# A decoder trunk: the sums of a short phase copied out by two engines and added later, more shared columns in the short phases, and gathered rows held five deep

## The chip, the cores and the metric

The kernel runs on one core of a Trainium2 chip, in one launch. The metric is the device time of that launch in microseconds (us). In this text TensorE is PE, VectorE DVE, ScalarE ACT and GpSimd POOL, as the profile abbreviates them.

## What is computed

One layer of a decoder for T = 256 tokens of width D = 2048, in float32: an attention mixer, then PEER, a layer that chooses 128 of 16,384 single-neuron experts for each token (8 heads, the best 16 each), then a norm. Only the last part of PEER matters here. The reference has it as

```
h = gelu(einsum('cd,chkd->chk', xc, u[ic]))
return einsum('chk,chkd->cd', gc * h, v[ic])
```

For each token this is a sum of 128 rows of V, each with a weight. The final norm of (input + this sum) is the output.

## The kernel before

All work up to the weights is done by earlier stages, which the change doesn't touch. What is left, called the **stage of V** here, computes the sum over experts of weight[token, expert] * V[expert, :] as a matrix product on PE.

**Columns.** The experts in use are sorted into lists of 128, called columns. A column is either *for one set* (its experts matter to one set of 128 tokens only) or *for both sets*. There are 78 one-set columns (HALVES), 26 for both (BOTH) and 2 more for both that are loaded without a list (LATE). `SEQ` (L1080 to 1093) is the order in which they are worked.

**Phases.** To have many one-set columns, the four quarters of 64 tokens are paired in three ways (`ORDERS`), one for each phase. Phases 0 and 1 have 12 one-set columns each, phase 2 has 54. The number m in L1081 is how many both-set columns a phase gets; they are spread evenly among its one-set columns. Before, m is 4, 4 and 16, and the 2 that are left come last. So phase 0 runs 3 one-set columns for each both-set column, phase 1 runs 4, phase 2 some 3.6. Phases 1 and 2 start with a both-set column, and each phase ends with one.

**One column.** POOL issues two indirect DMAs: `gather_v` (L1060) brings 128 rows of V (1 MiB) into one of 7 slots (`hg`), six columns ahead, and `gather_a` (L1068) brings the experts' weights (`ar`, 64 KB for one set and 128 KB for both) into one of 3 buffers, three columns ahead. Both are issued in program order, and each waits until the slot's last user is done. Then, for each half of the row (1024 wide), ACT rounds V to `hi` (L1150) and DVE takes `lo` = V − hi (L1151); ACT rounds the weights to `ah` (L1138), DVE takes `al` (L1140). `hi` and `lo` have 4 buffers each, that is two columns. PE (`v_products`, L1186 to 1188) multiplies ah·hi, ah·lo and al·hi into one bank of 512 columns: 12 products for one set of tokens (4 banks), 24 for both. There are 8 banks, named pv00 to pv11, pv02, pv03 and two that are named mm. The order of instructions on each engine is set by a scheduler which honours `high_priority` blocks; the parts of the next column are issued in such a block one column ahead.

**End of a phase.** When a bank has had its last product of phase 0 or 1, `put` (L1190) adds its two halves of 64 tokens to `acc` on DVE, two additions of 64x512 for each bank, 16 for each phase, also in a `high_priority` block. The next phase writes the same banks, so its first column, which is for both sets, waits for them. `finish` (L1198) and `last_norm` end the kernel after phase 2.

Of the kernel before, what the change touches and what calls it, by code (L numbers as in the profile page):

```python
# [10 lines left out]
F32 = mybir.dt.float32  # L11
# [4 lines left out]
AF = mybir.ActivationFunctionType  # L16
# [36 lines left out]
def decoder_trunk(ctx, tc, xT, g1, g2, gf, w_cols, w_v, w_out, w_q, u, v, subk, posk, posv,  # L53
# [4 lines left out]
    def f(ap):  # L58
        return ap.bitcast(F32)
# [561 lines left out]
    with ExitStack() as p3:  # L621
# [437 lines left out]
            else:  # L1059
                pool.indirect_dma_start(VR[n], None, v, bass.IndirectOffsetOnAxis(ap=idxV[:, n:n + 1], axis=0))  # L1060

        def gather_a(n):
            AR[n] = kp.tile([128, T], F32, name="ar", bufs=3)
            if n < 2 * KINDS[0][3]:
                src, dst = At.rearrange("r (t c) -> (r t) c", t=2), AR[n][:, 128 * sets[n][0]:128 * sets[n][0] + 128]
            else:
                src, dst = At, AR[n]
            pool.indirect_dma_start(dst, None, src, bass.IndirectOffsetOnAxis(ap=idxA[:, n:n + 1], axis=0))  # L1068
# [9 lines left out]
            two = [[n for n in range(HALVES) if phase[n] == ph and sets[n] == (t,)] for t in range(2)]  # L1078
            halves[ph] = [n for pair in zip(*two) for n in pair]
        SEQ, full = list(range(-LATE, 0)), list(range(HALVES, LIST))  # L1080
        for ph, m in ((0, 4), (1, 4), (2, BOTH - 10)):  # L1081

            h, first = halves[ph], 1 if ph else 0
            if first:
                SEQ.append(full.pop(0))
            m -= first
            for k in range(m):
                SEQ += h[len(h) * k // m:len(h) * (k + 1) // m] + [full.pop(0)]
            if ph == 2:
                SEQ += full  # L1090
            for n in SEQ:
                phase.setdefault(n, ph)
# [50 lines left out]
        def v_parts(n):  # L1143
            raw = VR.pop(n)
            res = []
            for h in range(2):
                hi = stream.tile([128, HALF], F32R, name="hi")
                lo = stream.tile([128, HALF], F32R, name="lo")
                r_ = raw[:, HALF * h:HALF * h + HALF]
                act.activation(hi, r_, AF.Copy)  # L1150
                dve.tensor_tensor(lo, r_, f(hi), op=OP.subtract)  # L1151
                res.append((hi, lo))
            return res

# [10 lines left out]
        with ExitStack() as pv_:  # L1165
# [15 lines left out]
            def v_products(n, t, c, ah, al, vv):  # L1181
# [5 lines left out]
                pe.matmul(ps, ah[:, tl], lo[:, cl], start=False, stop=False)  # L1187
                pe.matmul(ps, al[:, tl], hi[:, cl], start=False, stop=last)  # L1188

            def put(ph, t, c):  # L1190

                for k in range(2):
                    q = ORDERS[ph][2 * t + k]
                    s = acc[q // 2][64 * (q % 2):64 * (q % 2) + 64, 512 * c:512 * c + 512]
                    dve.tensor_tensor(s, sums[t, c][64 * k:64 * k + 64], s, op=OP.add)  # L1195

            scaled = {}

# [27 lines left out]

            sp.dma_start(gft, bass.AP(tensor=gf.tensor, offset=gf.offset, ap=[[0, 128], [1, D]]))
            for i, n in enumerate(SEQ):
                while fetched < min(i + AHEAD + 1, len(SEQ)):
                    gather_v(SEQ[fetched])  # L1230
                    fetched += 1
                if LATE <= i < len(SEQ) - 3:
                    gather_a(SEQ[i + 3])
                if LATE <= i + 1 < len(SEQ):
                    with tc.high_priority():
                        m = SEQ[i + 1]
# [5 lines left out]
                for t in sets[n]:  # L1242
                    for c in range(4):
                        v_products(n, t, c, ah, al, vv)
                        if phase[n] < 2 and n == ends[phase[n], t][-1]:
                            with tc.high_priority():
                                put(phase[n], t, c)
            with tc.high_priority():
                n_rest = nc.values_load(count[0:1, 0:1], min_val=0, max_val=NKEY * NKEY,  # L1249
                                        skip_runtime_bounds_check_because="a count of marked experts")  # L1250

            for t in range(2):
                for c in range(4):
# [126 lines left out]
```

## Time and profile before

| | |
|---|---|
| time, median of 3 runs | 1632.29 us (1630.9 to 1635.46) |
| time of the profiled execution | 1631.02 us |
| its span | 1629.3 us |
| PE busy | 1600.2 us, 98% of the span |
| DVE, ACT, POOL busy | 1243.8, 925.0, 407.8 us |
| first and last start of a product of the stage of V | 1226.62 and 1615.88 us |

The profiled execution's time stands 1.72 us above its span, and the median 1.27 us above that. In the views, a busy engine is one with an instruction in work; "[0.46 <-DVE acc L1195]" behind an instruction says that its engine was idle for 0.46 us before it, and that the addition into `acc` on line 1195 ended the wait. "x31" is a number of instructions.

### The profile page before, as it was taken

How to read it: one execution, taken by the hardware profiler on the slowest of the kernel's cores; microseconds unless marked ns; L12 is line 12 of the kernel's file. 1: busy time of each engine (PE TensorE's matmuls, PEld its weight loads, DVE VectorE, ACT ScalarE, POOL GpSimd, SP SyncE). 2: the span in 40 equal slices, each digit the busy share in tenths (PEclk: the TensorE clock that was granted, in tenths of full speed). 3: DMA queues.
4: the chain of work that ended last, by engine and by line, in shares of the span. 5: the costliest groups of instructions: out<-in, count | busy, mean ns of one | idle time of the engine just before them, and what ended most of it. 6: DMA issues, size and time to landing. Idle time of an engine off the chain costs nothing. (4 is left out here: it accounts for less than half of the span.)

```text
span 1629.3 us, 29096 instructions
## 1 busy us (share of the span) xinstructions
PE 1600.2 (98%) x11028; PEld 1436.2 (88%) x11028; DVE 1243.8 (76%) x2281; ACT 925.0 (57%) x1534; POOL 407.8 (25%) x390
## 2 busy tenths in 40 slices
PE   9999999999999999999999999999999998999996
PEld 8998889999999999999888888888887776788885
DVE  7797875678999996677687867765557887878776
ACT  6687775543454666566544444444446564766665
POOL 0010111100032310000211211121116575777661
PEclk9999999999999999999999999999999999999998
DMA  9544434555555576566999976677758786998892
GB/s 324 176 139 137 134 113 154 180 170 170 167 181 180 184 232 226 188 230 232 299 344 339 316 229 222 220 277 237 237 173 307 299 317 250 336 339 325 326 344 68
DMA packets 135423, 379.64 MB, mean 233 GB/s; under 512 B 12008, under 2 KB 67404, under 8 KB 119276
## 3 DMA queue, kind: packets, MB, share of 16 engines
q1 hardware_dynamic: 115596, 257.51, 47.8%
q0 software_dynamic: 19104, 119.16, 19.7%
q8 instruction: 88, 1.44, 0.3%
q10 hardware_dynamic: 576, 1.05, 0.2%
q14 instruction: 59, 0.48, 0.1%
HBM read 342.23 MB, written 35.44 MB: 232 GB/s over the span
## 5 line engine op out<-in xcount | busy, mean ns | idle before, releaser
L112 ACT ACTIVATE hi<-raw 128x1024 fp32r<-128x1024 f32 (+1 forms) x370 | 389.6, 1055 | 397.8 <-PE mm L645 158.1
L113 DVE TENSOR_TENSOR lo<-raw,hi 128x1024 fp32r<-128x1024 f32 (+1 forms) x370 | 461.3, 1249 | 181.3 <-ACT hi L112 179.5
L645 PE MATMUL mm<-X,hi 128*128 128x512 f32 x1216 | 429.5, 395 | 0.9 <-DVE hg L654 0.9
L161 PE MATMUL mm<-X,hi 128*128 128x256 f32 x1424 | 408.6, 287 | 0.0
L163 PE MATMUL mm<-X,lo 128*128 128x256 f32 x1424 | 403.0, 283 | 0.0
L162 PE MATMUL mm<-X,hi 128*128 128x256 f32 x1424 | 402.7, 283 | 0.0
L646 PE MATMUL mm<-X,lo 128*128 128x256 f32 x1216 | 339.7, 279 | 0.0
L1151 DVE TENSOR_TENSOR lo<-hg,hi 128x1024 fp32r<-128x1024 f32 x212 | 257.7, 1224 | 71.6 <-ACT hi L1150 62.7
L1150 ACT ACTIVATE hi<-hg 128x1024 fp32r<-128x1024 f32 x212 | 222.7, 1057 | 97.8 <-PE pv L1188 67.3
L645 PEld LDWEIGHTS mm<-X,hi 128*128 128x128 f32 x1216 | 227.8, 187 | 53.9 <-DVE hg L654 1.2
L161 PEld LDWEIGHTS mm<-X,hi 128*128 128x128 f32 x1424 | 269.7, 189 | 4.1 <-issue 3.9
L163 PEld LDWEIGHTS mm<-X,lo 128*128 128x128 f32 x1424 | 267.5, 188 | 1.0 <-DVE lo L113 0.6
L162 PEld LDWEIGHTS mm<-X,hi 128*128 128x128 f32 x1424 | 267.9, 188 | 0.5 <-issue 0.4
L646 PEld LDWEIGHTS mm<-X,lo 128*128 128x128 f32 x1216 | 228.0, 187 | 0.3 <-DVE lo L113 0.3
L655 POOL TENSOR_TENSOR hg<-hg,rB 128x256 f32<-128x256 f32 x74 | 70.8, 957 | 350.5 <-DVE hg L654 350.5
L1060 POOL DMA_INDIRECT hg<-in_v_dram,idxV x104 | 134.5, 1293 | 58.0 <-issue 24.3
L1187 PE MATMUL pv<-lo,ah 128*128 128x512 f32 x402 | 139.5, 398 | 0.9 <-DVE lo L1151 0.9
L1068 POOL DMA_INDIRECT ar<-At,idxA x104 | 119.6, 1150 | 76.0 <-DVE al L1140 46.6
L1188 PE MATMUL pv<-hi,al 128*128 128x512 f32 x402 | 135.9, 396 | 0.0
L1186 PE MATMUL pv<-hi,ah 128*128 128x512 f32 x402 | 124.7, 401 | 8.0 <-ACT ah L1138 4.7
L1186 PEld LDWEIGHTS pv<-hi,ah 128*128 128x128 f32 x402 | 75.9, 190 | 30.7 <-ACT ah L1138 7.9
L658 ACT ACTIVATE hg<-hg 128x256 f32<-128x256 f32 x128 | 52.3, 409 | 81.6 <-DVE hg L657 40.9
(293 smaller groups left out, 2247.8 us busy)
## 6 DMA issues: line engine op xcount, KB each, us to landing
raw<-in_u_dram SPq DMA_DIRECT2D x256, 512.0 KB, 4.7
raw<-in_w_cols_dram SPq DMA_DIRECT2D x42, 512.0 KB, 3.8
raw<-in_w_out_dram SPq DMA_DIRECT2D x32, 512.0 KB, 3.8
raw<-in_w_q_dram SPq DMA_DIRECT2D x32, 512.0 KB, 3.7
gs<-stg SPq DMA_DIRECT2D x16, 1024.0 KB, 4.7
gt<-gs SPq DMA_DIRECT2D x16, 1024.0 KB, 12.3
At<-a SPq DMA_DIRECT2D x31, 512.0 KB, 5.2
tb<-bd SPq DMA_DIRECT2D x16, 256.0 KB, 3.5
```

The costliest lines, as they stand in the source:

```text
L112: act.activation(hi[:, :n], raw[:, :n], AF.Copy)
L113: dve.tensor_tensor(lo[:, :n], raw[:, :n], f(hi[:, :n]), op=OP.subtract)
L161: pe.matmul(ps, hi[:, i, :], X[:, db, 0:T], start=db == 0, stop=False)
L162: pe.matmul(ps, hi[:, i, :], X[:, db, T:], start=False, stop=False)
L163: pe.matmul(ps, lo[:, i, :], X[:, db, 0:T], start=False, stop=db == DB - 1)
L645: pe.matmul(ps.rearrange("p a t -> p (a t)"), hi[:, i, :], X[:, db], start=db == 0, stop=False)
L646: pe.matmul(ps[:, 0], lo[:, i, :], X[:, db, 0:T], start=False, stop=db == DB - 1)
L1150: act.activation(hi, r_, AF.Copy)
L1151: dve.tensor_tensor(lo, r_, f(hi), op=OP.subtract)
L1186: pe.matmul(ps, ah[:, tl], hi[:, cl], start=first, stop=False)
L1187: pe.matmul(ps, ah[:, tl], lo[:, cl], start=False, stop=False)
L1188: pe.matmul(ps, al[:, tl], hi[:, cl], start=False, stop=last)
```

## The change

It has four parts.

1. `put` no longer adds. It copies the bank's two halves into a tile `part`, one half by DVE (L1201) and the other by ACT (L1199): 16 copies of 64x512 for each phase, 8 on each engine.
2. `add` (L1203) adds `part` to `acc` later, in four additions of 128x1024 for each phase. Each is issued on DVE right behind a `lo` of the next column, during a both-set column of the next phase that isn't its first.
3. m becomes 6, 6 and 12: phases 0 and 1 have six both-set columns each, so 2 to 2.4 one-set columns for each; phase 2 has 12 and the 2 last, with some 4.9 one-set columns between two.
4. The weights `ar` of all but the first three columns lie in 5 buffers in place of 3 and are gathered five columns ahead, and the gather of a step is issued ahead of that step's gather of V, no longer behind it.

```diff
--- before.py
+++ after.py
@@ -1059,8 +1059,8 @@
             else:
                 pool.indirect_dma_start(VR[n], None, v, bass.IndirectOffsetOnAxis(ap=idxV[:, n:n + 1], axis=0))
 
-        def gather_a(n):
-            AR[n] = kp.tile([128, T], F32, name="ar", bufs=3)
+        def gather_a(n, pool_=None):
+            AR[n] = kp.tile([128, T], F32, name="ar", bufs=3) if pool_ is None else pool_.tile([128, T], F32, name="ar", bufs=5)
             if n < 2 * KINDS[0][3]:
                 src, dst = At.rearrange("r (t c) -> (r t) c", t=2), AR[n][:, 128 * sets[n][0]:128 * sets[n][0] + 128]
             else:
@@ -1078,7 +1078,7 @@
             two = [[n for n in range(HALVES) if phase[n] == ph and sets[n] == (t,)] for t in range(2)]
             halves[ph] = [n for pair in zip(*two) for n in pair]
         SEQ, full = list(range(-LATE, 0)), list(range(HALVES, LIST))
-        for ph, m in ((0, 4), (1, 4), (2, BOTH - 10)):
+        for ph, m in ((0, 6), (1, 6), (2, BOTH - 14)):
 
             h, first = halves[ph], 1 if ph else 0
             if first:
@@ -1148,7 +1148,7 @@
                 lo = stream.tile([128, HALF], F32R, name="lo")
                 r_ = raw[:, HALF * h:HALF * h + HALF]
                 act.activation(hi, r_, AF.Copy)
-                dve.tensor_tensor(lo, r_, f(hi), op=OP.subtract)
+                st2["lo"] = dve.tensor_tensor(lo, r_, f(hi), op=OP.subtract)
                 res.append((hi, lo))
             return res
 
@@ -1187,12 +1187,22 @@
                 pe.matmul(ps, ah[:, tl], lo[:, cl], start=False, stop=False)
                 pe.matmul(ps, al[:, tl], hi[:, cl], start=False, stop=last)
 
+            part = vp.tile([128, 2, D], F32, name="part")
+            owed = []
+
             def put(ph, t, c):
 
-                for k in range(2):
-                    q = ORDERS[ph][2 * t + k]
-                    s = acc[q // 2][64 * (q % 2):64 * (q % 2) + 64, 512 * c:512 * c + 512]
-                    dve.tensor_tensor(s, sums[t, c][64 * k:64 * k + 64], s, op=OP.add)
+                for k, q in enumerate(ORDERS[ph][2 * t:2 * t + 2]):
+                    o = part[64 * (q % 2):64 * (q % 2) + 64, q // 2, 512 * c:512 * c + 512]
+                    s = sums[t, c][64 * k:64 * k + 64]
+                    if k:
+                        act.activation(o, s, AF.Copy)
+                    else:
+                        dve.tensor_copy(o, s)
+
+            def add(t, h):
+                s = acc[t][:, HALF * h:HALF * h + HALF]
+                dve.tensor_tensor(s, part[:, t, HALF * h:HALF * h + HALF], s, op=OP.add)
 
             scaled = {}
 
@@ -1226,11 +1236,12 @@
 
             sp.dma_start(gft, bass.AP(tensor=gf.tensor, offset=gf.offset, ap=[[0, 128], [1, D]]))
             for i, n in enumerate(SEQ):
+                if i >= LATE:
+                    for n_ in SEQ[i + (3 if i == LATE else 5):i + 6]:
+                        gather_a(n_, vp)
                 while fetched < min(i + AHEAD + 1, len(SEQ)):
                     gather_v(SEQ[fetched])
                     fetched += 1
-                if LATE <= i < len(SEQ) - 3:
-                    gather_a(SEQ[i + 3])
                 if LATE <= i + 1 < len(SEQ):
                     with tc.high_priority():
                         m = SEQ[i + 1]
@@ -1245,9 +1256,17 @@
                         if phase[n] < 2 and n == ends[phase[n], t][-1]:
                             with tc.high_priority():
                                 put(phase[n], t, c)
+                if phase[n] < phase[SEQ[i + 1]]:
+                    assert not owed
+                    owed = [(t, h) for t in range(2) for h in range(2)]
+                elif owed and len(sets[n]) == 2 and phase[SEQ[i - 1]] == phase[n]:
+
+                    with tc.issue_after(st2["lo"].ins):
+                        add(*owed.pop(0))
             with tc.high_priority():
                 n_rest = nc.values_load(count[0:1, 0:1], min_val=0, max_val=NKEY * NKEY,
                                         skip_runtime_bounds_check_because="a count of marked experts")
+            assert not owed
 
             for t in range(2):
                 for c in range(4):
```

How the instructions move on three engines' queues follows. A number behind a name tells tiles apart; in brackets is what an instruction waits for (DMASW and DMAHW are DMAs).

DVE at the end of phase 0, before. `pv..` and `mm` are the banks; lo_15363 and lo_15367 belong to the first column of phase 1.

```order
L1151 TENSOR_TENSOR lo_15367<-hg_4503,hi_15366 128x1024
L1195 TENSOR_TENSOR acc0_64<-pv00_14835,acc0_64 64x512
L1195 TENSOR_TENSOR acc1_65<-pv00_14835,acc1_65 64x512
...
L1195 TENSOR_TENSOR acc1_65<-pv03_14838,acc1_65 64x512
L1151 TENSOR_TENSOR lo_15420<-hg_4503,hi_15419 128x1024
L1195 TENSOR_TENSOR acc0_64<-mm_14841,acc0_64 64x512
L1195 TENSOR_TENSOR acc1_65<-mm_14841,acc1_65 64x512
L1195 TENSOR_TENSOR acc0_64<-mm_14842,acc0_64 64x512
L1195 TENSOR_TENSOR acc1_65<-mm_14842,acc1_65 64x512
L1140 TENSOR_TENSOR al_15428<-ar_15331,ah_15427 128x128
L1151 TENSOR_TENSOR lo_15424<-hg_4503,hi_15423 128x1024
```

The same place now; lo_15454 belongs to the first column of phase 1.

```order
L1151 TENSOR_TENSOR lo_15454<-hg_4503,hi_15453 128x1024
L1201 COPY part_14847<-pv00_14835 64x512
...
L1201 COPY part_14847<-pv03_14838 64x512
L1151 TENSOR_TENSOR lo_15507<-hg_4503,hi_15506 128x1024
L1201 COPY part_14847<-mm_14841 64x512
L1201 COPY part_14847<-mm_14842 64x512
L1140 TENSOR_TENSOR al_15515<-ar_15351,ah_15514 128x128
L1151 TENSOR_TENSOR lo_15511<-hg_4503,hi_15510 128x1024
L1151 TENSOR_TENSOR lo_15546<-hg_4503,hi_15545 128x1024
L1151 TENSOR_TENSOR lo_15550<-hg_4503,hi_15549 128x1024
L1140 TENSOR_TENSOR al_15554<-ar_15390,ah_15553 128x128
```

The sixteen additions are gone; eight copies stand in their place, six of them ahead of the next `lo`.

ACT at the same place, before, and PE where the first column of phase 1 ends. hi_15366 belongs to that first column; hi_15419 and hi_15423 to the next column, hi_15458, hi_15462 and ah_15466 to the one behind it.

```order
L1150 ACTIVATE hi_15419<-hg_4503 128x1024 [waits DMASW7_49,DVE_49,PE_49]
L1138 ACTIVATE ah_15427<-ar_15331 128x128 [waits DMASW6_49,DVE_49,PE_49]
L1150 ACTIVATE hi_15423<-hg_4503 128x1024 [waits DVE_49,PE_49]
L1150 ACTIVATE hi_15458<-hg_4503 128x1024 [waits DMASW1_49,DVE_49,PE_49]
L1138 ACTIVATE ah_15466<-ar_15360 128x128 [waits DMASW0_49,DVE_49,PE_49]
L1150 ACTIVATE hi_15462<-hg_4503 128x1024 [waits DVE_49,PE_49]
```

```order
L1186 MATMUL mm_14842<-hi_15366,ah_15370 128x512 [waits DVE_49]
L1187 MATMUL mm_14842<-lo_15367,ah_15370 128x512
L1188 MATMUL mm_14842<-hi_15366,al_15371 128x512
L1188 MATMUL pv00_14835<-hi_15419,al_15428 128x512 [waits DVE_49]
L1188 MATMUL pv01_14836<-hi_15419,al_15428 128x512
L1186 MATMUL pv10_14839<-hi_15458,ah_15466 128x512 [waits Activation_49]
L1186 MATMUL pv11_14840<-hi_15458,ah_15466 128x512
```

The same places now. hi_15453 belongs to the first column of phase 1, hi_15506 and hi_15510 to the next, hi_15545, hi_15549 and ah_15553 to the one behind it.

```order
L1199 ACTIVATE part_14847<-pv01_14836 64x512 [waits DVE_49]
L1199 ACTIVATE part_14847<-pv10_14839 64x512 [waits DVE_49]
L1138 ACTIVATE ah_15514<-ar_15351 128x128 [waits DMASW0_49,PE_49,Activation_49]
L1150 ACTIVATE hi_15510<-hg_4503 128x1024 [waits PE_49,Activation_49]
...
L1199 ACTIVATE part_14847<-mm_14841 64x512 [waits DVE_49]
L1150 ACTIVATE hi_15545<-hg_4503 128x1024 [waits DMASW7_49,PE_49,Activation_49]
L1199 ACTIVATE part_14847<-mm_14842 64x512 [waits DVE_49]
L1150 ACTIVATE hi_15549<-hg_4503 128x1024 [waits PE_49,Activation_49]
L1138 ACTIVATE ah_15553<-ar_15390 128x128 [waits DMASW2_49,DVE_49,PE_49]
```

```order
L1186 MATMUL mm_14842<-hi_15453,ah_15457 128x512 [waits Activation_49]
L1187 MATMUL mm_14842<-lo_15454,ah_15457 128x512
L1188 MATMUL mm_14842<-hi_15453,al_15458 128x512
L1186 MATMUL pv10_14839<-hi_15545,ah_15553 128x512 [waits Activation_49]
L1187 MATMUL pv10_14839<-lo_15546,ah_15553 128x512 [waits DVE_49]
L1186 MATMUL pv11_14840<-hi_15545,ah_15553 128x512
```

The copies have come among ACT's instructions, and of the second column behind the first the weights' `ah` has moved from the place between its two `hi` to the place behind both. On PE, two products that stood between the first column's last and the product that needs this `ah` are now elsewhere. The same pattern stands at the end of phase 1.

POOL at the start of the stage, before:

```order
L1068 DMA ar_14825<-At_10447,idxA_10460 128x256 [waits DMAHW4_49,DMAHW5_49,DMAHW3_49,DMAHW6_49,DMAHW2_49,DMAHW7_49,DMAHW1_49,DMAHW0_49]
L1068 DMA ar_14827<-At_10447,idxA_10460 128x256
L1068 DMA ar_14829<-At_10447,idxA_10460 128x256
L1060 DMA hg_4503<-in_v_dram,idxV_10461 128x2048 [waits DVE_49]
L1060 DMA hg_4503<-in_v_dram,idxV_10461 128x2048 [waits DMASW0_49,DVE_49]
L1060 DMA hg_4503<-in_v_dram,idxV_10461 128x2048 [waits DMASW1_49,DVE_49]
L1068 DMA ar_14911<-At_10447,idxA_10460 128x256 [waits DMASW4_49,DMASW2_49,DVE_49]
L1060 DMA hg_4503<-in_v_dram,idxV_10461 128x2048 [waits DMASW3_49,DVE_49]
L1068 DMA ar_14938<-At_10447,idxA_10460 128x256 [waits DMASW5_49,DVE_49]
L1060 DMA hg_4503<-in_v_dram,idxV_10461 128x2048 [waits DVE_49]
L1068 DMA ar_14965<-At_10447,idxA_10460 128x256 [waits DMASW6_49,DVE_49]
L1060 DMA hg_4503<-in_v_dram,idxV_10461 128x2048 [waits DMASW7_49,DVE_49]
```

and now:

```order
L1060 DMA hg_4503<-in_v_dram,idxV_10461 128x2048 [waits DVE_49]
L1060 DMA hg_4503<-in_v_dram,idxV_10461 128x2048 [waits DMASW0_49,DVE_49]
L1060 DMA hg_4503<-in_v_dram,idxV_10461 128x2048 [waits DMASW1_49,DVE_49]
L1068 DMA ar_14911<-At_10447,idxA_10460 128x256 [waits DMASW2_49,DMAHW1_49,DVE_49,DMAHW6_49,PE_49,Pool_49]
L1068 DMA ar_14913<-At_10447,idxA_10460 128x256 [waits DMASW3_49]
L1068 DMA ar_14915<-At_10447,idxA_10460 128x256 [waits DMASW4_49]
L1068 DMA ar_14942<-At_10447,idxA_10460 128x256 [waits DMASW5_49]
L1068 DMA ar_14971<-At_10447,idxA_10460 128x256 [waits DMASW6_49]
L1060 DMA hg_4503<-in_v_dram,idxV_10461 128x2048 [waits DMASW7_49,DVE_49]
L1060 DMA hg_4503<-in_v_dram,idxV_10461 128x2048 [waits DMASW0_49,DVE_49]
L1060 DMA hg_4503<-in_v_dram,idxV_10461 128x2048 [waits DMASW1_49,DVE_49]
```

Three V gathers stood between the third and the fourth gather of weights; now five gathers of weights go out together, and from then on each is one place ahead of its V.

## Rows read from the trace of the kernel before

**Rows 1.** The page, part 1: busy time of each engine.
```profile
PE 1600.2 (98%) x11028; PEld 1436.2 (88%) x11028; DVE 1243.8 (76%) x2281; ACT 925.0 (57%) x1534; POOL 407.8 (25%) x390
```

**Rows 2.** Windows: stretch, length, TensorE busy (products), clock, DMA share, GB/s.
```profile
1226.60:1295.50 68.90, 68.88 (x295) 1.00 0.90 342
1295.50:1306.50 11.00, 8.72 (x31) 1.00 0.17 74
...
1345.00:1350.00 5.00, 3.64 (x16) 1.00 0.95 365
...
1355.40:1370.50 15.10, 11.81 (x39) 0.89 0.29 102
...
1375.00:1381.00 6.00, 4.35 (x19) 1.00 0.80 279
```

**Rows 3.** Timeline of TensorE: start, us, what, [idle before <- releaser].
```profile
1226.62 0.50 PE L1186 MATMUL pv<-hi,ah 128*128 128x512 f32 x1 [1.56 <-ACT ah L1138]
...
1297.27 0.50 PE L1186 MATMUL pv<-hi,ah 128*128 128x512 f32 x1 [0.46 <-DVE acc L1195]
...
1347.01 0.50 PE L1186 MATMUL pv<-hi,ah 128*128 128x512 f32 x1 [1.36 <-ACT ah L1138]
...
1357.99 0.50 PE L1186 MATMUL pv<-hi,ah 128*128 128x512 f32 x1 [1.61 <-DVE acc L1195]
...
1377.73 1.67 PE L1186 MATMUL pv<-hi,ah 128*128 128x512 f32 x6 [1.65 <-ACT ah L1138]
...
1615.88 0.39 PE L1188 MATMUL mm<-hi,al 128*128 128x512 f32 x1
```

**Rows 4.** Timeline of VectorE at the end of phase 0.
```profile
1291.56 8.50 DVE L1195 TENSOR_TENSOR acc<-pv,acc 64x512 f32<-64x512 f32 x12
...
1304.07 0.29 DVE L1140 TENSOR_TENSOR al<-ar,ah 128x128 fp32r<-128x128 f32 x1
```

**Rows 5.** Timeline of GpSimd at the end of phase 0.
```profile
1292.58 0.94 POOL L1060 DMA_INDIRECT hg<-in_v_dram,idxV  x1 [0.30 <-issue]
1304.63 1.69 POOL L1068 DMA_INDIRECT ar<-At,idxA  x1 [11.11 <-DVE al L1140]
```

**Rows 6.** Timeline of ScalarE around both phase ends.
```profile
1292.25 1.06 ACT L1150 ACTIVATE hi<-hg 128x1024 fp32r<-128x1024 f32 x1 [2.26 <-PE pv L1188]
...
1349.71 0.42 ACT L1138 ACTIVATE ah<-ar 128x256 fp32r<-128x256 f32 x1 [2.35 <-DMA ar<-At,idxA]
...
1370.52 2.96 ACT L1150 ACTIVATE hi<-hg 128x1024 fp32r<-128x1024 f32 x3 [0.15 <-PE pv L1188]
```

**Rows 7.** Groups by line, stage of V: xcount | busy us, mean ns | idle before.
```profile
L1151 DVE TENSOR_TENSOR lo<-hg,hi 128x1024 fp32r<-128x1024 f32 x212 | 257.7, 1224 | 71.6 <-ACT hi L1150 62.7 <-issue 5.5 <-DMA hg<-in_v_dram,idxV 2.1
L1150 ACT ACTIVATE hi<-hg 128x1024 fp32r<-128x1024 f32 x212 | 222.7, 1057 | 97.8 <-PE pv L1188 67.3 <-DMA hg<-in_v_dram,idxV 8.4 <-issue 7.7
...
L1138 ACT ACTIVATE ah<-ar 128x128 fp32r<-128x128 f32 x94 | 27.8, 305 | 36.8 <-PE mm L1187 22.7 <-DMA ar<-At,idxA 8.3 <-DVE lo L1151 1.3
...
L1195 DVE TENSOR_TENSOR acc<-pv,acc 64x512 f32<-64x512 f32 x24 | 16.5, 689 | 0.6
```

**Rows 8.** Groups by line, whole program: copies out of the sums' memory.
```profile
L503 ACT ACTIVATE pt<-tp 128x512 f32<-128x512 f32 x16 | 9.5, 596 | 5.3 <-PE tp L498 5.1
...
L506 DVE COPY pca<-tp 15x128 f32<-15x128 f32 x16 | 4.3, 269 | 0.0
```

**Rows 9.** Windows, all engines: PE, PEld, DVE, ACT, POOL, clock, DMA share, GB/s.
```profile
1300.00:1305.00 5.00, 3.74 (x13) 2.23 (x14) 4.88 (x8) 0.14 (x1) 0.37 (x1) 1.00 0.00 0
1357.00:1358.00 1.00, 0.01 (x1) 0.01 (x1) 0.95 (x3) 0.00 (x0) 0.73 (x1) 1.00 0.09 37
1361.00:1362.00 1.00, 1.00 (x4) 0.71 (x4) 0.99 (x2) 0.00 (x0) 0.00 (x0) 0.50 0.61 254
1388.00:1606.00 218.00, 217.99 (x935) 175.48 (x934) 168.79 (x193) 149.64 (x194) 147.04 (x121) 1.00 0.84 310
1455.00:1460.00 5.00, 5.00 (x23) 4.01 (x22) 3.87 (x5) 2.26 (x4) 4.09 (x4) 1.00 1.04 401
```

## The prediction

> **What bounds the kernel now.** The page's first part comes first: PE is busy for 1600.2 us of the span of 1629.3, 98% [rows 1]. Nothing in the change alters the number of products, so all it can give back is PE's idle time, and I look for that in the stage of V alone, since PE's order before it is the same. The timeline of PE gives the stage's two ends: the first product starts at 1226.62, the last at 1615.88 [rows 3], 389.26 us for 78 × 12 + 28 × 24 = 1608 products. The pace without waits is read from a long stretch in which PE never stops: 935 products in 218.0 us [rows 9], 0.2332 us each. 1607 steps at this pace are 374.7 us, so 14.5 us at most are lost.
>
> The windows show where. Length less products × 0.2332: 3.8 us at the end of phase 0, 1.3 at 1345, 6.0 at the end of phase 1, 1.6 at 1375, together 12.6; the first stretch of 68.9 us loses nothing [rows 2]. I take **13.5**, between the two counts. The causes are in the timelines:
> - End of a phase: DVE makes twelve additions in 8.50 us [rows 4], 0.71 each, and PE waits for `acc` before each bank, 0.46 us at 1297.27 and 1.61 at 1357.99 [rows 3]. In the 15.1 us around the second end the granted clock is 0.89 on average [rows 2], with 0.50 at 1361 [rows 9]: of the 6.0, 0.11 × 15.1 = 1.7 us are the clock's.
> - Behind each end: POOL stands 11.11 us at its next gather of weights until `al` is done [rows 5], and the DMAs move nothing at 1300 to 1305 [rows 9]. Then ACT waits 2.35 us for `ar` [rows 6] and PE for ACT's `ah`, 1.36 us at 1347.01 and 1.65 at 1377.73 [rows 3].
>
> **The change, part by part.**
>
> *Copies for additions.* Each phase's end takes 16 additions of 689 ns [rows 7] from DVE, 11.0 us, and puts 8 copies on DVE and 8 on ACT. No copy of this shape is in the trace. DVE: a 128-wide copy out of a bank takes 269 ns [rows 8] and a 512-wide addition from a bank 689. These are the bounds; I take 0.70, the row of the same shape. ACT: 512 wide out of a bank is 596 [rows 8], a 128-wide `ah` 305 [rows 7]; I take 0.60, by the same reason. So DVE has 5.6 us where it had 11.0, but the banks still come free one by one: by the order, ACT's copy of a bank waits for DVE's copy of the same bank, and PE for ACT's.
>
> I walked the three queues with these prices, T being the first product of the phase's last column. By the order of its products its eight banks end at T+3.2 (the 14th product) to T+5.8. DVE's copies end at T+3.9, then every 0.7. PE uses up one bank of the next phase's first column in three products, 0.70 us, the same pace, so it hardly falls behind: 0.05 us at the first bank. ACT has two `hi` and an `ah` among its copies, and pv11's comes 0.4 us late because `ah` and a `hi` (0.30 + 1.06, [rows 7]) stand ahead of it. Then, at T+12, comes **a new wait that the order shows**: the second `hi` of the second column behind needs the buffer that PE's last product of the first column (mm, al) still reads; this column's `ah` now stands *behind* that `hi` on ACT, where it stood ahead of it; and PE's very next product needs this `ah`. So PE ends its product (0.39, [rows 3]), ACT makes `hi` (1.06) and `ah` (0.30), and only then PE goes on: 1.75 less the 0.23 that a product takes anyway, 1.5 us, and some 0.1 for the handing over. One end costs 0.05 + 0.4 + 1.6 = 2.1 us; the second end has the same order, so **4.2 us** in all, for 3.8 + 6.0 = 9.8 before (of the windows).
>
> *Additions beside both-set columns.* Eight of 128x1024 on DVE, at `lo`'s 1224 ns for this shape [rows 7]. In phase 1 a group of 2 one-set columns and a both-set column is 11.2 us of PE (48 products); DVE has 6 `lo` (7.3), `al` four times by the one-set price (1.2) and the addition, 9.7 in all. In phase 2 a group of 5 and one is 84 products, 19.6 us, against 12 `lo` (14.7), `al` (2.0) and an addition, 17.9. Both fit; I cost them at **nothing**. Where the cover is gone each delays the next `al` by at most 1.2 us.
>
> *Where both-set columns go.* The products are the same. Phase 0's group falls from 14.0 to 11.2 us of PE, phase 2's rises from 15.7 to some 19.4 with six columns' gathers in place of 4.6. POOL's two issues for a column are 2 × 147.04 / 121 = 2.4 us [rows 9], with 0.3 of issue before each [rows 5] 3.0; 6 × 3.0 = 18.2 of 19.6 us. The DMAs: a one-set column is 1.114 MB, a both-set one 1.180; 54 and 12 of them are 74.3 MB in 54 × 2.8 + 12 × 5.6 = 218 us, 340 GB/s (before, with 16: 79.0 MB in 241, 328). The first 69 us of the stage moved 342 at a share of 0.90 with PE losing nothing [rows 2], and five us reached 401 [rows 9]. I cost this at **nothing**, with its price among the rivals.
>
> The Trainium skill, "DMA: Bandwidth & Descriptors", section "Bandwidth", has 341 GB/s for transfers of 1 MB issued from GpSimd and some 358 as what a core gets from its memory, which speaks against the change. At 341, 74.3 MB would take 217.9 us: no loss, but no reserve either. The 401 in a stretch of five us [rows 9] is above both figures.
>
> *Weights five columns ahead.* A row that comes late is now late by the same wait of POOL, but it is wanted two columns, 5.6 us or more, further on; the waits were 1.36 and 1.65. POOL's stand shrinks too, since DVE's queue ahead of `al` is 5.4 us shorter; ACT's copies ahead of `ah` give some 2 back, so to 7 or 8 us. So the 1.3 and 1.6 go: **nothing left**. At the start five gathers of weights go out ahead of the fourth V, 3 × 1.5 = 4.5 us later for that V; six columns have been asked for by then, so it isn't waited for.
>
> **Sum.** 13.5 lost now, 4.2 then: 9.3 us less. The profiled execution is 1631.0, so 1621.7; the median of the runs stands 1.3 above that, so **1623.0 us**. About 0.3%, 4.9 us, is what a measurement of this kernel can tell from no change.
>
> **The rivals.**
>
> 1. *The end of a phase costs more than walked* (4 to 7 us gained; 1625 to 1628). For: an idle of 1.61 us was followed by clock 0.50, 1.7 us lost; I forecast idles of 1.5. Against: of the four idles of 1.36 to 1.65 us in the rows only one was. Two such falls, 3.4 us, leave 5.9; copies at 0.8 us in place of 0.7 would delay the eighth bank by 0.8 more.
> 2. *The waits nearly vanish* (12 to 13.5 gained; about 1619). DVE copies at 0.27 and PE is slowed by something else before it comes to the late `ah`. Against it: the wait on `ah` hangs on the order, not on the copies' price.
> 3. *V's gathers fall behind in phase 2*, the rival that ends slower. Its place is the run of five one-set columns, 5 × 2.8 us of PE for 5 × 1.114 MB, 398 GB/s, with the ring of seven as the only store. At a rate r PE waits 74.3 MB / r − 218 us less the store, six columns or some 20 us less the 8 in which POOL stands at the phase's end. At 310, the mean of the long stretch [rows 9], if that were the ceiling: 240 − 218 − 12 = 9.5, which is all that the change gains, so **310 GB/s decides**; at 300 it is 17 and the time 1640. For: share 0.84 there, already near full; POOL has 1.4 us to spare in 19.6. Against: that mean holds some 15 us at the end in which nothing is left to gather; 342 over 69 us is shown, and 401 at best.
> 4. *The weights' new order brings nothing*: the gathers stand behind another wait, and the 2.9 us of waits stay: 6.4 gained, 1626.
>
> **How the numbers follow.** Forecast (7 to 12 gained, 1620.3 to 1625.3) 0.60, all faster. Rival 1: 0.18, of which 0.12 faster by over 0.3% and 0.06 within it. Rival 2: 0.05, faster. Rival 3: 0.13, of which 0.02 faster, 0.05 within, 0.06 slower. Rival 4: 0.04, of which 0.03 faster, 0.01 within. Together 0.82 faster, 0.12 the same, 0.06 slower. The range is 1618.5 (every wait gone: 13.5 + 0.3) to 1628.5 (rival 1's end); it leaves out most of rival 3. The bounds of the copies' prices lie inside it.
>
> **What would show it.** Right: PE's last product starts some 9 us earlier, near 1606.5; behind the first column of phases 1 and 2 PE waits 1.3 to 1.7 us for ACT's `ah` (L1138), and elsewhere at a phase's end under 0.6 at a time, for ACT's copies (L1199); copies of 0.70 on DVE and 0.60 on ACT; no wait of ACT for `ar` behind a phase's end; POOL stands at most 8 us; PE busy throughout phase 2's windows. Wrong: PE or ACT waiting for DMAs of V (`hg`) in phase 2 (rival 3); a clock near 0.5 behind both ends (rival 1); no wait for `ah` after the first columns (rival 2).

## The result and the profile after

The changed kernel takes 1618.16 us (median of 4 runs, 1617.34 to 1621.59); the kernel before, with a fourth run now, 1633.88 (1630.9 to 1637.22). The ratio is 0.9914, with a 95% interval of 0.9900 to 0.9929: faster by 0.7 to 1.0%, some 14 us. The forecast was faster by 9.3, at 1623.0: the direction is right, the gain was larger, and the median stands 0.3 us below the lower end of the range.

The page's part 1 for the changed kernel answers to [rows 1]:

```profile
PE 1599.5 (99%) x11028; PEld 1440.2 (89%) x11028; DVE 1241.2 (77%) x2277; ACT 935.3 (58%) x1554; POOL 404.2 (25%) x390
```

The waits of TensorE in the stage of V (engine, line, what it waited for: us in total, times, longest) are two, where the kernel before had twelve:

```profile
PE pv L1186 <- ACT ah L1138: 1.6, 1, 1.6
PE pv L1186 <- ACT part L1199: 0.2, 1, 0.2
```

The first is the one at the stage's start, which the change doesn't touch [rows 3]. In the timeline of TensorE (start, us, what, idle before) the stage's two ends answer to those of [rows 3]; between them stand the only wait of over 0.1 us and the place behind the first column of phase 1 where the prediction had put its new wait:

```profile
1230.15 0.50 PE L1186 MATMUL pv<-hi,ah 128*128 128x512 f32 x1 [1.56 <-ACT ah L1138]
...
1311.73 0.50 PE L1186 MATMUL pv<-hi,ah 128*128 128x512 f32 x1 [0.18 <-ACT part L1199]
...
1316.97 0.39 PE L1186 MATMUL mm<-hi,ah 128*128 128x512 f32 x1
1317.20 0.40 PE L1187 MATMUL mm<-lo,ah 128*128 128x512 f32 x1
1317.43 0.39 PE L1188 MATMUL mm<-hi,al 128*128 128x512 f32 x1
1317.66 0.44 PE L1186 MATMUL pv<-hi,ah 128*128 128x512 f32 x1
...
1606.40 0.40 PE L1188 MATMUL mm<-hi,al 128*128 128x512 f32 x1
```

From 1230.15 to 1606.40 the stage takes **376.25 us**, where it took 389.26: 13.0 less. 1607 steps at 0.2332 us are 374.7, so 1.5 us are still lost, where 14.5 were. The two ends of phases cost 0.7 and 0.5 us of that: one product starts 0.07 late at the first bank, one 0.34 or 0.21 late at the fourth, and the product behind each of these loses 0.1 more.

The span of this execution is only 9.4 us shorter than before's, close to the forecast, but by chance. The stage starts 3.5 us later than before, in a program that is the same up to there. The windows (length, then TensorE, its weight loads, DVE, ACT, POOL; clock, DMA share, GB/s) show why, and in the last row phase 2's pace:

```profile
44.00:48.00 4.00, 4.00 (x36) 4.00 (x35) 3.93 (x12) 2.91 (x7) 0.00 (x0) 1.00 0.91 257
52.00:56.00 4.00, 4.00 (x20) 4.00 (x20) 1.59 (x2) 2.24 (x2) 0.00 (x0) 0.50 0.19 75
56.00:60.00 4.00, 4.00 (x29) 4.00 (x27) 2.35 (x9) 3.50 (x11) 0.00 (x0) 0.72 0.45 135
1420.00:1560.00 140.00, 140.00 (x602) 112.80 (x601) 114.64 (x130) 99.16 (x130) 101.66 (x87) 1.00 0.93 351
```

At 52 to 56 us the granted clock is 0.50, half speed, and over 56 to 60 it is 0.72. In the profiled execution of before it is 1.00 there:

```profile
52.00:56.00 4.00, 4.00 (x36) 4.00 (x35) 2.76 (x7) 3.88 (x9) 0.00 (x0) 1.00 0.16 41
```

Of the thirteen profiled executions of this study six have a clock of 0.91 over the stretch from 40 to 80 us and one has 0.96, in kernels with and without the change's parts, whose programs are the same up to there. The runs of the changed kernel go with it: 1621.59, the profiled one, has a mean clock of 0.995, the three of 1617.34 to 1618.98 have 0.997. Runs of one kernel are some 3 to 7 us apart, and as far as the profiles show, much of that lies far ahead of the change. So below each kernel is judged by its stage of V in one profiled execution, with the ratio of the runs beside it.

### The profile page after: what moved, and what is told of

Same layout as the page of the kernel before. It is cut to its first block, busy times and chain, and to the rows that moved or that the text cites. A ratio compares the mean times of both kernels' runs of the same rounds, so it can differ in the third digit from the quotient of the medians.

```text
span 1619.9 us, 29124 instructions
## 1 busy us (share of the span) xinstructions
PE 1599.5 (99%) x11028; PEld 1440.2 (89%) x11028; DVE 1241.2 (77%) x2277; ACT 935.3 (58%) x1554; POOL 404.2 (25%) x390
## 4 chain that ended last, share of the span: by engine, by line
PE 94%; DVE 3%; ACT 1%; DMA 0%; issue 0%; SPq 0%; DVEq 0%; ACTq 0%
PE mm L645 18%; PE mm L161 10%; PE mm L162 10%; PE mm L163 10%; PE mm L646 9%; PE pv L1186 6%; PE pv L1188 6%; PE pv L1187 6%; PE mm L1186 2%; PE mm L1188 2%; PE mm L1187 2%; PE mm L561 2%; PE mm L562 2%; PE mm L563 2%; PE tp L814 2%; PE av L533 1%
## 5 line engine op out<-in xcount | busy, mean ns | idle before, releaser
L1060 POOL DMA_INDIRECT hg<-in_v_dram,idxV x104 | 131.0, 1259 | 50.2 <-issue 24.0
L1188 PE MATMUL pv<-hi,al 128*128 128x512 f32 x402 | 137.3, 396 | 0.0
```

## The experiments

The change has three separable parts here: the copies with the later additions (**put**), the both-set columns, 6, 6 and 12 (**m**), the weights five ahead (**rows**). All eight combinations of the three are known from two kernels and six runs:

| kernel | put | m | rows | stage of V, us | ratio to before, 95% interval |
|---|---|---|---|---|---|
| before | | | | 389.26 | 1 |
| b_m | | x | | 390.95 | 1.0011 (1.0000 to 1.0022) |
| b_rows | | | x | 383.15 | 0.9962 (0.9948 to 0.9976) |
| b_put | x | | | 380.28 | 0.9941 (0.9927 to 0.9956) |
| b_put_m | x | x | | 382.99 | 0.9965 (0.9952 to 0.9979) |
| rows_m | | x | x | 384.85 | 0.9960 (0.9946 to 0.9974) |
| put_rows | x | | x | 376.24 | 0.9912 (0.9897 to 0.9927) |
| the change | x | x | x | 376.25 | 0.9914 (0.9900 to 0.9929) |

Each stage is the start of its last product less that of its first, from the timeline of TensorE.

### One part alone

**b_m**, only the both-set columns:

```diff
-        for ph, m in ((0, 4), (1, 4), (2, BOTH - 10)):
+        for ph, m in ((0, 6), (1, 6), (2, BOTH - 14)):
```

> The kernel before with the change's third part alone: six both-set columns in phases 0 and 1, the additions at the phase's end and the rows of weights as before. Theory A (VectorE is what is short in phases 0 and 1: a one-set column takes 2 x 1.224 + 0.29 = 2.74 us of it beside 2.8 of TensorE, a both-set column 3.0 beside 5.6, so only both-set columns let it and the gathers catch up): the waits at the two ends stay, some 9 us, and the two waits on late rows of weights (1.36 and 1.65) go: 2 to 4 us faster. Theory B (each part removes only the waits that it names): no change, within 1 us.

Neither: 1.7 us *longer*. The waits (all engines, the stage) show the price:

```profile
ACT ah L1138 <- DMA ar<-At,idxA: 29.4, 20, 4.1
...
PE pv L1186 <- ACT ah L1138: 6.6, 10, 1.6
```

TensorE waits ten times for `ah`, once at the start and nine times in phase 2, 0.41 to 0.90 us each, because ACT waits for weights that haven't landed, 29.4 us in all (13.0 in the kernel before). The longer runs of one-set columns that this part makes in phase 2 make three buffers of weights too few.

The total hides that theory A's forecast for phases 0 and 1 came true: between the two ends TensorE waits for no `ah`, and the second end now starts like the first:

```profile
1383.40 0.50 PE L1186 MATMUL pv<-hi,ah 128*128 128x512 f32 x1 [0.46 <-DVE acc L1195]
```

Counted as length less products × 0.2332, the stage up to and with the second end loses 8.3 us in place of 12.2, and phase 2 behind it loses 7.9 in place of 2.3.

**b_rows**, only the weights' gathers as in the change:

```diff
+AR[n] = kp.tile([128, T], F32, name="ar", bufs=3) if pool_ is None else pool_.tile([128, T], F32, name="ar", bufs=5)
...
+                if i >= LATE:
+                    for n_ in SEQ[i + (3 if i == LATE else 5):i + 6]:
+                        gather_a(n_, vp)
```

> The kernel before with the change's fourth part alone: weights in five buffers, gathered five columns ahead. Theory A and theory B: the two waits on late rows go, 2 to 3 us faster, the ends of the phases stay as they are. A third possibility: what is late is the gather queue as a whole, and ScalarE then waits for V in place of the weights: no change.

More than both theories: 6.1 us less. The waits of 1.36 and 1.65 are gone, but so is what made the second end of a phase dearer than the first. TensorE's rows at the first end (1297) and the second (1357, 1362):

```profile
1297.27 0.50 PE L1186 MATMUL pv<-hi,ah 128*128 128x512 f32 x1 [0.47 <-DVE acc L1195]
...
1357.25 0.50 PE L1186 MATMUL pv<-hi,ah 128*128 128x512 f32 x1 [0.46 <-DVE acc L1195]
...
1362.77 0.50 PE L1186 MATMUL mm<-hi,ah 128*128 128x512 f32 x1 [0.69 <-DVE acc L1195]
```

The 1.61 us of before at 1357.99, the halved clock behind it [rows 3, 9] and this wait for `lo` of before

```profile
1366.95 0.73 PE L1187 MATMUL pv<-lo,ah 128*128 128x512 f32 x2 [0.88 <-DVE lo L1151]
```

are gone; the first end's 0.46 stands in their place, as in b_m. So of the 6.0 us that the second end cost [rows 2], only some 3.8 were the additions'; the rest was late weights and what followed from them. By the same count as above, the 6.1 us are 1.6 in phase 1, 2.3 at the second end and 2.2 behind it.

**b_put**, only the copies and the later additions, with two additions beside each of two both-set columns:

```diff
-                        add(*owed.pop(0))
+                        for _ in range(2):
+                            add(*owed.pop(0))
```

This diff is against the change; its third and fourth part are undone.

> The kernel before with the change's first two parts alone: copies by two engines, additions of 128x1024 later, here two beside each of two both-set columns, since phase 1 has only two that serve. Theory A: the ends fall from 9.8 us of waits to 1, but in phase 1 VectorE has 39.2 for lo, 5.8 for al, 4.9 for additions and 5.6 for copies, 55.5 us in 56 of TensorE, so part comes back as waits for lo and al: 5 to 8 us faster. Theory B: 9 us faster, with the two waits on late rows left.

9.0 us less, so the total fits theory B. The waits that are left stand in phase 1:

```profile
1328.98 1.19 PE L1186 MATMUL pv<-hi,ah 128*128 128x512 f32 x4 [0.28 <-ACT ah L1138]
...
1335.46 1.69 PE L1186 MATMUL pv<-hi,ah 128*128 128x512 f32 x6 [0.62 <-ACT hi L1150]
...
1350.97 0.50 PE L1186 MATMUL pv<-hi,ah 128*128 128x512 f32 x1 [1.05 <-ACT ah L1138]
...
1361.05 1.12 PE L1186 MATMUL pv<-hi,ah 128*128 128x512 f32 x2 [0.54 <-ACT ah L1138]
```

These are 2.5 us, by their size what theory A expected of a short DVE. put_rows, below, tells the two apart.

### Two parts

**b_put_m**, the change without its fourth part, and then **put_rows**, the change without its third, with the two additions of b_put, and **rows_m**, the change without the first two.

> The change without its fourth part: weights in three buffers, three columns ahead, as before. Theory A: GpSimd stands only some 5 us and the gathers have both-set columns to catch up in, so no row is late: as fast as the whole change, 12 to 14 us faster than before. Theory B: the two waits on late rows stay: 9 to 11 us faster.

Both theories fail: it is 2.7 us *longer* than the copies alone. TensorE's waits are those of b_m, about one for each run of one-set columns in phase 2:

```profile
1402.55 0.73 PE L1186 MATMUL pv<-hi,ah 128*128 128x512 f32 x2 [1.13 <-ACT ah L1138]
...
1465.76 0.50 PE L1186 MATMUL pv<-hi,ah 128*128 128x512 f32 x1 [0.41 <-ACT ah L1138]
...
1486.04 0.50 PE L1186 MATMUL pv<-hi,ah 128*128 128x512 f32 x1 [0.41 <-ACT ah L1138]
...
1506.32 0.50 PE L1186 MATMUL pv<-hi,ah 128*128 128x512 f32 x1 [0.41 <-ACT ah L1138]
```

So with three buffers the third part costs 1.7 to 2.7 us, and the fourth part gives 6.7 on top of the others. The cost is a balance here too: phase 1 has no wait left, so the stage up to and with the second end loses 1.4 us in place of b_put's 5.4, and phase 2 loses 6.9 in place of 0.1.

> The change without its third part: four both-set columns in phases 0 and 1 as before, two additions of 128x1024 beside each of two both-set columns of the next phase. By the stages of the runs so far: the copies alone gave 9.0 us, the weights five ahead alone 6.1, of which some 3 were late weights behind the copies' places too. Theory A (VectorE has 55.5 us of work in phase 1's 56 of TensorE): waits for hi, lo and al in phase 1 of 1 to 3 us stay, a stage of 377 to 380 us, 9.5 to 12 us faster than before, and the third part is worth the rest. Theory C (the third part brings nothing of its own but the places for the additions, since late weights were all that made phase 1 wait): a stage of 376, as fast as the whole change, 13 to 14 us faster.

Theory C: 376.24, the change's stage to 0.01 us. TensorE waits for nothing in phase 1, although the both-set columns are as in the kernel before and DVE has all its additions to make. So the 2.5 us of b_put were late weights, DVE wasn't short, and **with weights five ahead the third part gives nothing of its own**. Its places for single additions aren't needed either, since two beside one column cost nothing here.

> The kernel before with the third and the fourth part, without the copies. Phase 2's longer runs of one-set columns cost nothing with weights five ahead, by both theories, so as the fourth part alone: 5 to 7 us faster, a stage of 383, with the additions' 3.6 us of waits at each end. If the third part has a price of its own (gathers of V), it is slower than the fourth part alone by 2 us or more.

384.85, so 4.4 us less than before (by the runs 0.4%, 6.5 us), but 1.7 more than with the fourth part alone: TensorE waits 0.99 for `ah` and 0.22 for `hi` once, behind the second end. By the runs the two can't be told apart (0.9960 and 0.9962). It is no trend through phase 2, and the same wait stands in all_dve at the same place. What ACT's `ah` waits for there stays open.

### Two engines or one

**all_dve**, both halves copied by DVE:

```diff
-                    if k:
-                        act.activation(o, s, AF.Copy)
-                    else:
-                        dve.tensor_copy(o, s)
+                    dve.tensor_copy(o, s)
```

> The change with all sixteen copies of a phase on VectorE. A copy measured 0.64 us there, an addition 0.71. If the pace at which VectorE frees the banks is what TensorE waits for, 16 x 0.64 + 2.4 for two lo = 12.6 us from the first bank's end to the last, and TensorE's two columns over these banks leave some 8.4: 3 us of waits at each end, as with the additions, 5 to 7 us slower than the change. If instead ScalarE's copies, each behind VectorE's of the same bank, were the longer chain, no slower than the change.

8.6 us slower than the change, a stage of 384.86 (ratio 0.9973, 0.9960 to 0.9985, the change's 0.9914). TensorE's waits are those of b_rows for the additions, 0.46, 0.46, 0.22, 0.69 and 0.46 at each end to a hundredth, in all

```profile
PE mm L1186 <- DVE part L1198: 2.3, 4, 0.7
PE pv L1186 <- DVE part L1198: 2.3, 6, 0.5
```

so copying early instead of adding brings nothing by itself: rows_m, which is this kernel with additions at the phase's end, has 384.85. VectorE's timeline shows why; its twelve copies of six banks take as long as the twelve additions did [rows 4]:

```profile
1302.12 8.50 DVE L1198 COPY part<-pv 64x512 f32<-64x512 f32 x12 [0.55 <-PE pv L1188]
```

That is 1.42 us for each bank, 0.71 from one copy to the next and not the 0.64 of the expectation. With two engines DVE's copy of a bank takes 0.68, and ACT's 0.59 runs beside DVE's next, so the banks come free in about half the time. Of the 8.6 us the two ends are 6.9, within the 5 to 7 expected; the other 1.7 are the wait behind the second end that rows_m has too.

### Which property of the weights' gathers

**order3**: three buffers and three ahead, but issued ahead of the step's V, as in the change. **rows4**: four buffers, four ahead. The diff is order3's against b_put_m:

```diff
+                if LATE <= i < len(SEQ) - 3:
+                    gather_a(SEQ[i + 3])
                 while fetched < min(i + AHEAD + 1, len(SEQ)):
                     gather_v(SEQ[fetched])
                     fetched += 1
-                if LATE <= i < len(SEQ) - 3:
-                    gather_a(SEQ[i + 3])
```

> The change with three buffers of weights, three columns ahead, but each gather issued ahead of its step's gather of V as in the change. Where the weights were gathered behind V this kernel had a stage of 382.99 us, with five buffers 376.25. If it is the place in the queue that made weights late: 376 to 377, as the change. If it is the depth (a gather can't be issued before al of three columns back is done, then it shares the DMAs with 1 MB gathers): 382 to 384, no better than without the change's fourth part.

> The change with four buffers of weights, four columns ahead, in place of five. If depth is what counts, one more buffer gives 2.8 us more from issue to use in a run of one-set columns, and the waits left with three were 0.4 to 1.1 us each: 376 to 377, as fast as the change. If the fifth is needed: 378 to 381.

order3 has a stage of 382.95, like b_put_m's 382.99 (ratio 0.9963), and nearly the same waits:

```profile
ACT ah L1138 <- DMA ar<-At,idxA: 22.5, 13, 4.0
...
PE pv L1186 <- ACT ah L1138: 5.9, 9, 1.6
```

rows4 has 376.93, with one wait of 0.41 us late in phase 2 (ratio 0.9934, 0.9918 to 0.9950; its profiled execution lost its time before the stage, which starts at 1232.12 after a clock of 0.96 and 0.91 in the first 80 us). Depth is what counts (buffers and columns ahead, which go together here), four is nearly enough, and with three the place in the queue does nothing.

### How far the third part can go

**m888**: eight both-set columns in each phase, as a test of the rival that ends slower.

```diff
-        for ph, m in ((0, 6), (1, 6), (2, BOTH - 14)):
+        for ph, m in ((0, 8), (1, 8), (2, BOTH - 18)):
```

> The change with eight both-set columns in each phase, so phase 2 runs 7.7 one-set columns between two. 54 x 1.114 + 8 x 1.180 = 69.6 MB in 196 us of TensorE, 355 GB/s. If gathers of V can't hold a rate over some 350 GB/s (the change moved 351 in a stretch of 140 us of phase 2), TensorE waits for V late in phase 2: at 345 GB/s 202 us less a store of some 12, so still no wait; at 320, 9 us. A theory in which the queue of issues binds (3.0 us for a column on GpSimd beside 2.8 of TensorE) gives waits only when the run is longer than the ring's seven columns: within 1 us of the change.

A stage of 387.75 (ratio 0.9993, 0.9982 to 1.0003): nearly the whole gain is lost, by five waits of 0.4 to 1.9 us for `ah` between 1547 and 1587. The windows show the DMAs full until 1530, and then 40 us with 130 products, so 9.7 us lost, 6.0 in waits and the rest by a clock of 0.91 on average:

```profile
1450.00:1530.00 80.00, 80.00 (x344) 64.45 (x344) 69.89 (x81) 58.26 (x78) 63.26 (x55) 1.00 0.99 380
1540.00:1580.00 40.00, 33.99 (x130) 25.94 (x129) 25.18 (x30) 21.70 (x31) 22.98 (x19) 0.91 0.75 262
```

That looks like the gathers falling behind, but the timelines of TensorE and ACT at the first of these waits say otherwise:

```profile
1544.09 1.09 PE L1188 MATMUL pv<-hi,al 128*128 128x512 f32 x4
1547.02 0.50 PE L1186 MATMUL pv<-hi,ah 128*128 128x512 f32 x1 [1.83 <-ACT ah L1138]
```

```profile
1544.76 2.00 ACT L1150 ACTIVATE hi<-hg 128x1024 fp32r<-128x1024 f32 x2 [1.26 <-PE pv L1188]
1546.67 0.49 ACT L1138 ACTIVATE ah<-ar 128x128 fp32r<-128x128 f32 x2
```

ACT is idle for TensorE, not for a DMA: the first of two `hi` waits until TensorE has released a buffer, and `ah`, which TensorE needs next, stands behind both. On ACT's timeline late in phase 2, three or four `hi` run between two `ah`. So the run after it changes this order alone.

**m888_ah**: the same, and each `ah` forced ahead of its column's `hi`.

```diff
-                        held[m] = v_parts(m)
                         pa[m] = a_parts(m)
+                        with tc.issue_after(st2["ah"].ins):
+                            held[m] = v_parts(m)
```

> Eight both-set columns in each phase, as in the run before, and each column's ah forced ahead of its two hi on ScalarE. Theory D (the 11.5 us that eight cost are the order's: late in phase 2 ah stands behind hi that wait for TensorE to free their buffers, and TensorE waits for that ah): the waits at 1547 to 1587 and the halved clock behind them go, a stage of 376 to 378, 1617 to 1620. Theory E (gathers fall behind at 355 GB/s and the order only showed where): the waits come back in another place, as ScalarE waiting for V or for weights, and the time stays at 1628 to 1632.

A stage of 378.82 (ratio 0.9952, 0.9935 to 0.9969; this profiled execution again has a clock of 0.91 at 40 to 80 us): theory D by its mechanism, though the stage is 0.8 above its 378 and the median of the runs, 1625.22, some 5 above its 1620. The five waits are gone and the DMAs carry the demand of 355 GB/s for 130 us with TensorE at work for 129.82 of them:

```profile
1410.00:1540.00 130.00, 129.82 (x555) 103.72 (x554) 112.32 (x129) 91.27 (x124) 101.42 (x85) 1.00 0.95 357
```

The stage is 2.6 us longer than the change's. Some 1.1 of this is the forced order's price at the ends of the phases, where ACT's copies now come later; the rest is short waits in phase 2, of which the largest is the last row's:

```profile
PE pv L1186 <- ACT part L1199: 1.7, 2, 0.8
...
PE mm L1186 <- ACT hi L1150: 0.2, 1, 0.2
```

## Why the prediction was right or wrong

- **Where the time lay.** Right: the stage of V alone, and all waits of before but the first are gone. I took 13.5 us as lost; the upper count of 14.5 is the one that fits, since 13.0 came back and 1.5 are left, 1.2 of it at the two ends. The stage alone would have put the median at 1632.29 − 13.0 = 1619.3, inside the range; that it lies 0.3 under it comes from ahead of the stage, where runs differ by more than that, and is chance.
- **The copies' prices.** Right: 0.68 us on DVE (forecast 0.70), 0.59 on ACT (0.60), the additions 1.22 (1.224). The groups by line in the stage (count, busy us, mean ns, idle before):

```profile
L1205 DVE TENSOR_TENSOR acc<-part,acc 128x1024 f32<-128x1024 f32 x8 | 9.7, 1217 | 0.0
L1201 DVE COPY part<-pv 64x512 f32<-64x512 f32 x12 | 7.5, 677 | 0.8 <-PE pv L1188 0.7
L1199 ACT ACTIVATE part<-pv 64x512 f32<-64x512 f32 x12 | 6.5, 588 | 0.1
```

- **The banks' chain.** Right: 0.07 us at the first bank and 0.34 or 0.21 at the fourth, for 0.05 and 0.4. That both engines are needed for it is shown by all_dve.
- **The new wait at T+12: this step failed.** I had 1.6 us at each end, because ACT's second `hi` of a column would wait for the buffer that TensorE's last product of the first column (mm, al) still reads. ACT's timeline at that place:

```profile
1313.42 1.06 ACT L1150 ACTIVATE hi<-hg 128x1024 fp32r<-128x1024 f32 x1
1314.51 0.59 ACT L1199 ACTIVATE part<-mm 64x512 f32<-64x512 f32 x1
1316.29 1.06 ACT L1150 ACTIVATE hi<-hg 128x1024 fp32r<-128x1024 f32 x1 [1.19 <-PE pv L1188]
1317.26 0.29 ACT L1138 ACTIVATE ah<-ar 128x128 fp32r<-128x128 f32 x1
```

  That `hi` starts at 1316.29, behind a product of `pv` on L1188. TensorE's last three products of mm start at 1316.97 to 1317.43 (above), so the `hi` doesn't take that buffer. I had assumed that buffers are handed out in turn; the order of instructions shows only which engine is waited for, not which product. `ah` is done at 1317.55 and TensorE goes on at 1317.66, in step. Two times 1.6 us fewer waits, 3.2 in all, are most of the 3.7 by which the gain was forecast too small; that 14.5 us were lost before, and not 13.5, is 1.0 more, and the banks' waits and the rest cost some 0.5 more than forecast. The mechanism itself exists: in m888 the same wait, `ah` behind a `hi` that waits for TensorE, cost up to 1.93 us at a time, and the lowered clock on top.
- **The weights five ahead: mis-sized.** I gave them the two waits of 1.36 and 1.65, 2.9 us; alone they give 6.1, since the second end's dearer part was late weights too. I had put this part to the copies, so the sum of the two was not off by it.
- **Where both-set columns go at nothing.** Right for the whole change (0.01 us between it and put_rows), but only because the fourth part is there. With three buffers it gains at the second end and loses more in phase 2, 1.7 us on balance alone and 2.7 with the copies. I looked for its price at V's gathers; it was at the weights' buffers, which I had costed only at a phase's end.
- **Additions beside both-set columns at nothing.** Right, and even with two beside one (put_rows).
- **GpSimd's stand** shrank from 11.11 us [rows 5] to 5.43 and 4.59, less than the 7 to 8 forecast:

```profile
1313.23 1.69 POOL L1068 DMA_INDIRECT ar<-At,idxA  x1 [5.43 <-DVE al L1140]
...
1380.62 1.68 POOL L1068 DMA_INDIRECT ar<-At,idxA  x1 [4.59 <-DVE al L1140]
```

- **The rivals.** The second, that the waits nearly vanish (0.05), is what happened, but not by its reason: the copies are no faster than forecast. The third didn't come at 340 GB/s (phase 2 moved 351 over 140 us with TensorE never idle), nor at 355; 310 as the rate that decides was never near, since 380 was carried over 80 us in m888. The Trainium skill, "DMA: Bandwidth & Descriptors", section "Bandwidth", has 341 GB/s for one such transfer and some 358 as a core's limit, which the same section also gives as what each core gets when both of a pair stream; this kernel runs on one. The measured 380 lies above both, and it decides here. The fourth is refuted by b_rows. For the first there was no halved clock behind either end of the changed kernel.

## What to carry to other kernels

A part that is free in the whole change can cost time without another part: longer runs of short steps were covered only because the small gathers had more buffers, and only runs of each part alone and of pairs show that. When an engine waits for a small operand, look first at how deep its buffers are and what stands ahead of it in its producer's queue; a full DMA share close by, as the 0.99 in m888, is no proof that DMAs are the cause. Before costing a wait for a buffer, find in a trace which reader releases it.

## What was not expected of the hardware

The granted clock fell to 0.50 for some microseconds at about 52 us, far ahead of all that was changed, in some executions and not in others of what is there the same program, and cost some 3.5 us: the changed kernel's stage starts at 1230.15, b_rows' at 1226.61. In the stage of V a wait of 1.61 us in the kernel before was followed by the same [rows 3, 9], while b_m, b_rows, rows_m and all_dve, with ten waits of 0.22 to 0.70 at their phases' ends, show 1.00 there throughout. In m888 two of the five waits for `ah` were followed by it, those of 1.83 us at 1547.02 and of 1.93 at 1567.56; behind the one of 0.88 at 1555.32 the clock stayed at 1.00:

```profile
1548.00:1551.00 3.00, 3.00 (x9) 2.33 (x8) 0.61 (x3) 0.00 (x0) 1.91 (x3) 0.50 0.99 360
1556.00:1560.00 4.00, 4.00 (x19) 3.21 (x18) 1.86 (x4) 1.06 (x2) 2.83 (x2) 1.00 0.81 280
1569.00:1571.00 2.00, 2.00 (x6) 1.55 (x5) 0.24 (x1) 0.00 (x0) 1.70 (x2) 0.50 0.96 270
```

The length of a wait alone doesn't decide it: in the kernel before, the wait of 1.65 us at 1377.73 was followed by 1.00 and the one of 1.61 was not [rows 2, 3, 9]. What does was not tried and stays open.

That gathers of 1 MB for one core move 380 GB/s over 80 us beside a TensorE that never stops was not expected either; 340 had looked near the limit.
